# First half of the output product between the halves of the attention-output product, and a new order inside an attention turn

## The chip, the cores and the metric

The kernel runs on one core of one Trainium2 chip, as one program and one launch. The metric is device time in microseconds (us), from runs of the whole kernel. Engines are named as in the profile: PE is TensorE, DVE is VectorE, ACT is ScalarE, POOL is GpSimd, SP issues most transfers.

## The reference, cut to what matters

Two transformer-like layers, one after the other, on a sequence of 1024 tokens by 1024 features, in float32. The change lies in the first:

```python
u = rms_norm(x) @ w_in                   # v, b, c, z, q, k, v_a, z_a, gates
y_a = conv_branch(...) @ w_conv_out      # "co"
o = sliding_window_attention(q, k, v, sinks) * silu(z_a)
y_b = o @ w_attn_out                     # "ao"
merged = sigmoid(g_a) * y_a + sigmoid(g_b) * y_b
x = x + merged @ w_out                   # "wo"
```

The attention has 16 query heads and 4 key/value heads of 64, blocks of 128 queries, each looking at its own block and the one before. The second layer (pooling and gated linear attention, cross attention, a feed-forward part) begins with an RMS norm of x and stays as it is.

## The kernel before, in words

**Numbers.** Each float32 operand of a large product is held as a rounded high part and a low part (the rest); a product is three matmuls (`mm3`, L380): high by high, high by low, low by high. ACT makes high parts, DVE low ones. Activations lie with features on partitions, as 8 tiles of 128 by 512 for each half of the tokens (h = 0, 1). A `dense` (L385) is one weight page of 1024 by 128 times one half: 8 x 3 matmuls into one of three banks `mm`.

**Weights.** `_stream` (L79) lists the weight pages in the order of use, and `Weights` (L229) walks it: SP loads raw pages (`wr`, two buffers, L241), `pf` (L258) has ACT make `wh` (L281, two buffers) and notes the low part, `flush` has DVE make it (`wl`, L345). `get` takes a page and starts the one after.

**Ticks.** All other work lies in Python generators in the list `side`. `tick()` (L178) makes the open low parts of weights and then takes each generator one `yield` further. A `dense` ticks after half of its matmuls, and the loop around it ticks again at its end, so a product is two ticks. This sets the order of instructions on every engine; each engine takes its own in that order and waits where an operand isn't there.

**z and the sums.** After the first norm, `first_two` (L515) multiplies the first two z pages with both halves, then two more z pages follow (L913). Beside that, `sums` (L446) makes the four sums T1 to T4 of the tiles, which the later two-page products of seven block products (`wino`, L398) need; with `fast=True` two of three of its 18 steps end in a yield.

**Attention.** A unit is one pair of key/value heads, one block of queries and two of four query heads of each: 32 units, 16 a half. `attention()` (L1159) gives one turn a tick. In turn i it emits `expo` of unit i-1 (ACT: 4 exponentials, `pr`, L1100), `values` of i-4 (PE into the one bank `o`, L1151; DVE multiplies by the gate, L1155), on odd i `differ` of i-3 (a difference of two value blocks, POOL), `finish` of i-1 (DVE: sum `den` and reciprocal, L1106, L1107; POOL: the division of `pr`, L1108), `turn` of i-2 (PE: 4 transposes, L1128; ACT: `pch`, L1130; DVE: `pcl`, L1131; POOL: masked copies, L1138) and `scores` of i (PE, L1078, into both banks `s`; ACT and DVE copy to `pr`, L1082, L1083; DVE: maximum and scale, L1085 to L1091). Outputs that are complete are split into `oh`, `ol` (L376, L377). Attention starts beside "co" (L1216) and ends beside the first half of "ao".

**ao and wo.** "ao" (L1239) goes over both halves, 8 pages each; behind each product DVE multiplies by the gate (L1250), adds the conv branch (L1251) and ACT and DVE split the merged tile (`mgh`, `mgl`). Gate and conv tiles are loaded one product ahead on SP (`g<-gbd`, `g<-mcd`, L1201). `x` is loaded again on POOL's queue, its first half beside the second half of "ao", its second half behind it. `residual` (L1257) then does "wo": h = 0, 8 products, each added to x (L1267), squared by ACT and summed by POOL (`Norm`, L554), then `norm_thread` (L611) for that half in `side`: beside the second half it makes `xn` (L622), `xnh` and `xnl` a tick; then h = 1.

Of the kernel before, what the change touches and what calls it, by code (L numbers as in the profile page):

```python
# [11 lines left out]
ALU = mybir.AluOpType  # L12
# [6 lines left out]
KT = 8  # L19
# [59 lines left out]
def _stream():  # L79
    st = [("v", 0), ("v", 1)]  # L80
    st += [("z", 0, j) for j in range(4)]
    st += [("pair", ("z", 1, j), ("z", 1, j + 1)) for j in (0, 2)]
    st += [("pair", ("q", p, j), ("q", p, j + 1)) for p in range(2) for j in (0, 2)]
    st += [("pair", ("gb", m), ("gb", m + 1)) for m in range(0, KT, 2)]
    for c in range(KT):
        st += [("pair", ("cc", c), ("cv", c)), ("pair", ("cz", c), ("cb", c))]
    st += [("pair", ("ga", m), ("ga", m + 1)) for m in range(0, KT, 2)]
    st += [("co", m) for m in range(KT)] * 2
    st += [("ao", m) for m in range(KT)] * 2
    st += [("wo", m) for m in range(KT)] * 2  # L90
    st += [("p2", 0)]
    for p in range(2):
        st += [("q2", p), ("k2", p), ("v2", p, 0), ("v2", p, 1)]
    st += [("r2", 0), ("r2", 1), ("p2", 1), ("p2", 2), ("r2", 2), ("p2", 3), ("r2", 3)]
    st += [("wo2", m) for m in range(KT)] * 2
    for m in range(KT):
        st += [("xq", m), ("mk", m), ("mv", m // 4, m % 4)]
    st += [("xq", m) for m in range(KT)]
    st += [("xo", m) for m in range(KT)] * 2
    for f in range(NFF):  # L100
        st += [("fg", f), ("fv", f)] if f < FF_STD else [("pair", ("fg", f), ("fv", f))]
    for g in range(len(FF_GROUPS)):
        st += [("fd", g, m) for m in range(KT)]
    return st
# [12 lines left out]
def _body(es, tc, nc, wp, vec, xT, memT, gk2, pw, cst, out, dbg):  # L117
# [19 lines left out]
    def tp(s, dt=F32, shape=(P, HT)):  # L137
        return tpool.tile(list(shape), dt, name=nm(s), tag="tp")
# [68 lines left out]
    class Page:  # L207
        def __init__(self, his, los):
            self.his, self.los, self.n = his, los, 1024 // len(his)
# [233 lines left out]
        for tag in ("s", "s", "o"):  # L443
            T.matmul(ps(tag), hi[:, :P], hi, start=True, stop=True)

    def sums(t, X, hts, fast=False):  # L446


        at = {"T1": (0, 0), "T2": (4, 1), "T3": (0, 1), "T4": (4, 0)}
        order = ("T1", "T2", "T3", "T4")  # L450
        his, los = {}, {}

        def u(name, k):
            return t[at[name][0] + k, at[name][1]]

        def hi(name, k):
            his[name, k] = hts[name](name, F32R)
            S.copy(his[name, k], u(name, k))

        def lo(name, k):  # L460
            los[name, k] = hts[name](name, F32R)
            V.tensor_tensor(los[name, k], u(name, k), f(his[name, k]), ALU.subtract)
            if k == 3:
                X[name] = [(his[name, i], los[name, i]) for i in range(4)]

        for i in range(18):
            if 2 <= i and i - 2 < 16:
                j = i - 2
                lo(order[j // 4], j % 4)
            if 1 <= i < 17:  # L470
                j = i - 1
                hi(order[j // 4], j % 4)
            k = i % 4
            if i < 4:
                V.tensor_tensor(u("T1", k), u("T3", k), u("T1", k), ALU.subtract)
                V.tensor_tensor(u("T3", k), u("T3", k), u("T2", k), ALU.subtract)
            elif i < 8:
                V.tensor_tensor(u("T2", k), u("T2", k), u("T1", k), ALU.subtract)
            elif i < 12:
                while (4 + k, 0) not in t:  # L480
                    yield
                V.tensor_tensor(u("T4", k), u("T4", k), u("T2", k), ALU.subtract)
            if not fast or i % 3:
                yield

    def reload(items, s, first=4, per=2, lag=3):

# [24 lines left out]
            evac(dense(w, act, h), h)  # L512
            tick()

    def first_two(na, nb, act, ea, eb, spare=False):  # L515

        a = W.get(na)
        ea(dense(a, act, 0), 0)
        tick()
        b = W.get(nb, pf=False)  # L520
        eb(dense(b, act, 0), 0)
        tick()
        while None in [x[1] for x in act]:
            tick()
        if spare:
            W.pf(spare=True)
        o = dense(a, act, 1)
        if not spare:
            W.pf()
        ea(o, 1)  # L530
        tick()
        eb(dense(b, act, 1), 1)
        tick()
# [18 lines left out]


    class Norm:  # L554
        def __init__(self):
            self.acc = None

        def add(self, x, eng=V):
            sq = tp("sq")[:, :x.shape[-1]]
            S.activation(sq, x, AF.Square)  # L560
            if self.acc is None:
                self.acc = sq
            else:
                eng.tensor_tensor(self.acc, self.acc, sq, ALU.add)  # L564
# [70 lines left out]
    def grid(n):  # L635
        return [[None, None] for _ in range(n)]
# [204 lines left out]
    def hT_sums():  # L841
        for k in range(4):
            ht_in(k, hp)
        while None in [x[1] for x in hT]:
            yield
        side.append(ht_rest())
        yield from sums(ht, XB, {"T1": hp, "T2": hp, "T3": hq, "T4": hq}, True)

    def ht_rest():
        while len(kd) < 8 or len(vd) < 4:  # L850
# [58 lines left out]
        wino((na, nb), X, lambda x: evac(0, 0, x), c22, c12, lambda y: evac(1, 0, y))  # L909

    side.append(hT_sums())
    first_two(("z", 0, 0), ("z", 0, 1), hT, *[lambda o, h, j=j: z_out(0, j, h, o) for j in range(2)])
    for j in (2, 3):  # L913
        both(("z", 0, j), hT, lambda o, h: z_out(0, j, h, o))
    while "T1" not in XB:
# [243 lines left out]
    def attention():  # L1159
        units = [Unit(p, h, b, half) for h in range(2) for p in range(2) for b in range(4) for half in range(2)]  # L1160
        n = len(units)
        todo = []
        dv = None
        for _ in range(5):
            yield
        for i in range(n + 4):
            if 0 <= i - 1 < n:
                units[i - 1].expo()
            if 0 <= i - 4 < n:
                units[i - 4].values(dv)  # L1170
                if i % 8 == 3:
                    u = units[i - 4]
                    todo += [(u.p, j, u.h) for j in range(4)]
            if i % 2 and 0 <= i - 3 < n and units[i - 3].n:
                dv = units[i - 3].differ()
            if 0 <= i - 1 < n:
                units[i - 1].finish()
            if 0 <= i - 2 < n:
                units[i - 2].turn()
            if i < n:  # L1180
                units[i].scores()
            if i in (8, 16):
                side.append(att_in(i // 16, 1))
            if todo:
                p, j, h = todo.pop(0)
                osp[4 * p + j][h] = split(oT[p][j][h], "o")
            yield
        while todo:
            p, j, h = todo.pop(0)
            osp[4 * p + j][h] = split(oT[p][j][h], "o")  # L1190
            yield
# [42 lines left out]
        gate_in(gbi, gbd, m, h)  # L1234
        gate_in(cin, mcd, m, h)

    xs = grid(KT)
    ao_in(0, 0)
    for h in range(2):  # L1239
        for m in range(KT):  # L1240
            w = W.get(("ao", m))
            ao_in(m + 1, h)
            if h and m >= 4:
                for i in (0, 1):
                    load_x(0, 2 * (m - 4) + i, nc.gpsimd)
            while None in [osp[c][h] for c in range(KT)]:
                tick()
            o = dense(w, osp, h)
            t = gbi[m, h]
            V.tensor_tensor(t, t, o, ALU.mult)  # L1250
            V.tensor_tensor(t, t, cin[m, h], ALU.add)  # L1251
            mgs[m][h] = split(t, "mg")
            tick()
    for kt in range(KT):
        load_x(1, kt, nc.gpsimd)

    def residual(wname, act, gname, nxt, fast=True, norm=None, between=None, away=None, back=None):  # L1257

        for h in range(2):
            nrm = Norm()  # L1260
            for m in range(KT):
                w = W.get((wname, m))
                if back is not None:
                    for i in range(3) if m == h == 0 else (m + 2,):
                        back(*((h, i) if i < KT else (h + 1, i - KT)))
                o = dense(w, act, h)
                V.tensor_tensor(xs[m][h], xs[m][h], o, ALU.add)  # L1267
                nrm.add(xs[m][h], V if m == KT - 1 else G)
                tick()
            if norm is not None:  # L1270
                side.append(norm([nrm.acc], h))
            else:
                side.append(norm_thread([nrm.acc], xs, gname, h, nxt, fast and h == 1, 1 + (h and not fast),
                                        away))
            if between is not None and h == 0:
                between()

    gr = tp("gr", shape=(P, KT, 16))  # L1280
# [1 line left out]
    gw = tp("gw", F32R, (P, KT, 32))  # L1282
    S.copy(gw[:, :, 0:16], gr)
    V.tensor_tensor(gw[:, :, 16:32], gr, f(gw[:, :, 0:16]), ALU.subtract)
    xn = grid(KT)
    residual("wo", mgs, "norm_mix", xn)


    gl = [None, None]
# [773 lines left out]
```

## Time and profile before

| | us |
|---|---|
| median of 3 runs | 2409.21 |
| lowest, highest run | 2407.96, 2411.95 |
| the profiled execution | 2407.34 |
| its span, first to last instruction | 2405.6 |
| PE busy in the span | 2366.1 |
| DVE, ACT, POOL busy | 1487.5, 1009.5, 577.8 |
| mean granted clock of PE | 0.995 of full |

Busy times overlap, and PE's ends are modelled, so a stretch is judged by the idle time before a matmul and by what ended it. In a row of the timeline the first number is the start from the span's beginning, the second how long it lasted; in brackets stands the engine's idle time before it and what ended that. [...]

### The profile page before, as it was taken

The page shows a single profiled execution, that of the slowest core. Times are in us where ns is not written, and L with a number is a line of the kernel's source. Part 1 is how long each engine was busy: PE and PEld are TensorE (multiplying, and loading weights), DVE is VectorE, ACT ScalarE, POOL GpSimd, SP SyncE. Part 2 cuts the span into 40 slices and gives each one's busy share as a digit, 9 for nine tenths or more (in the row PEclk, how much of TensorE's full clock was granted, in tenths as well). Part 3 has the DMA queues.
Part 4 walks back from the last instruction along what each step waited for, and adds up shares of the span by engine and source line. Part 5 has one row for each costly group of instructions (what it writes and reads, how often), then busy time and mean ns, then how long its engine had stood idle before and what let it go on. Part 6 is the DMA issues. An engine that isn't in the chain of part 4 may idle for free.

```text
span 2405.6 us, 30929 instructions
## 1 busy us (share of the span) xinstructions
PE 2366.1 (98%) x11574; PEld 1952.4 (81%) x11574; DVE 1487.5 (62%) x2317; ACT 1009.5 (42%) x1869; POOL 577.8 (24%) x554
## 2 busy tenths in 40 slices
PE   8999999999999999999999999999999999999998
PEld 8788888888887787887888888888888888888887
DVE  7744346666537997555445556455798888873435
ACT  5444433333346664334322334443555555552112
POOL 3235433333303552121001120001233333310003
PEclk9999999999999999999999999999999999999999
DMA  4533322122247534621100245322422222245222
GB/s 166 181 126 135 124 84 71 62 70 70 84 170 260 184 135 150 210 90 50 39 28 29 88 127 179 97 83 91 160 88 79 79 84 79 93 139 167 84 78 93
DMA packets 107510, 264.97 MB, mean 110 GB/s; under 512 B 12096, under 2 KB 14560, under 8 KB 107360
## 3 DMA queue, kind: packets, MB, share of 16 engines
q1 hardware_dynamic: 104880, 256.70, 31.3%
q0 software_dynamic: 1936, 5.77, 0.7%
q8 instruction: 91, 1.49, 0.2%
q10 hardware_dynamic: 544, 0.52, 0.1%
q14 instruction: 59, 0.48, 0.1%
HBM read 203.18 MB, written 59.77 MB: 109 GB/s over the span
## 4 chain that ended last, share of the span: by engine, by line
PE 88%; DVE 6%; ACT 3%; DMA 1%; issue 1%; POOL 0%; SPq 0%; DVEq 0%; POOLq 0%; ACTq 0%
PE psmm L381 14%; PE psmm L383 13%; PE psmm L382 13%; PE pss L410 6%; PE pss L412 5%; PE pss L411 5%; PE psmm L410 4%; PE psmm L412 4%; PE psmm L411 4%; PE pst L410 2%; PE pst L412 2%; PE pst L411 2%; PE pso L410 2%; PE pso L412 2%; PE pso L411 2%
## 5 line engine op out<-in xcount | busy, mean ns | idle before, releaser
L345 DVE TENSOR_TENSOR wl<-wr,wh 128x1024 fp32r<-128x1024 f32 (+1 forms) x147 | 180.3, 1226 | 97.7 <-ACT wh L281 97.5
L410 PE MATMUL pss<-T,wsh 128*128 128x512 f32 x588 | 232.0, 395 | 0.1
L412 PE MATMUL pss<-T,wsl 128*128 128x512 f32 x588 | 230.1, 391 | 0.0
L411 PE MATMUL pss<-T,wsh 128*128 128x512 f32 x588 | 229.4, 390 | 0.0
L330 DVE TENSOR_TENSOR wsl<-ws,wsh 128x512 fp32r<-128x512 f32 x196 | 208.3, 1103 | 33.4 <-ACT wsh L312 32.4
L564 POOL TENSOR_TENSOR sq<-sq,sq 128x512 f32<-128x512 f32 (+1 forms) x58 | 70.9, 1222 | 608.7 <-ACT sq L560 605.1
L281 ACT CAST wh<-wr 128x1024 fp32r<-128x1024 f32 (+1 forms) x147 | 148.2, 1008 | 149.7 <-PE psmm L382 128.5
L298 POOL TENSOR_TENSOR ws<-wr 128x512 f32<-128x512 f32 x49 | 69.8, 1425 | 567.5 <-DMA wr<-in_wp_dram 459.0
L381 PE MATMUL psmm<-xnh,wh 128*128 128x512 f32 x448 | 179.3, 400 | 5.0 <-ACT wh L281 5.0
L383 PE MATMUL psmm<-xnh,wl 128*128 128x512 f32 x448 | 175.9, 393 | 0.7 <-DVE wl L345 0.7
L382 PE MATMUL psmm<-xnl,wh 128*128 128x512 f32 x448 | 175.5, 392 | 0.0
L410 PE MATMUL psmm<-xnh,wh 128*128 128x512 f32 x392 | 153.9, 393 | 0.0
L412 PE MATMUL psmm<-xnh,wl 128*128 128x512 f32 x392 | 153.2, 391 | 0.0
L411 PE MATMUL psmm<-xnl,wh 128*128 128x512 f32 x392 | 152.6, 389 | 0.0
L410 PEld LDWEIGHTS pss<-T,wsh 128*128 128x128 f32 x588 | 110.4, 188 | 25.6 <-DVE cb L990 2.4
L412 PEld LDWEIGHTS pss<-T,wsl 128*128 128x128 f32 x588 | 110.3, 188 | 25.2
L411 PEld LDWEIGHTS pss<-T,wsh 128*128 128x128 f32 x588 | 110.4, 188 | 23.6
L383 PE MATMUL psmm<-fh,wl 128*128 128x512 f32 (+1 forms) x300 | 116.0, 387 | 1.1 <-DVE wl L345 1.1
L560 ACT ACTIVATE sq<-x 128x512 f32<-128x512 f32 (+1 forms) x80 | 47.1, 588 | 164.7 <-DVE x L1267 110.4
L381 PE MATMUL psmm<-fh,wh 128*128 128x512 f32 (+1 forms) x300 | 115.9, 386 | 0.0
L382 PE MATMUL psmm<-fl,wh 128*128 128x512 f32 (+1 forms) x300 | 115.9, 386 | 0.0
L302 DVE TENSOR_TENSOR wl<-wr,wh 128x1024 fp32r<-128x1024 f32 x49 | 66.0, 1346 | 70.8 <-ACT wh L296 70.8
(453 smaller groups left out, 6231.7 us busy)
## 6 DMA issues: line engine op xcount, KB each, us to landing
wr<-in_wp_dram SPq DMA_DIRECT2D x238, 512.0 KB, 3.7
act<-fa SPq DMA_DIRECT2D x44, 256.0 KB, 2.1
fr<-act SPq DMA_DIRECT2D x44, 256.0 KB, 4.4
wr<-in_wp_dram SPq DMA_DIRECT2D x24, 384.0 KB, 3.1
xd<-x SPq DMA_DIRECT2D x32, 256.0 KB, 4.4
x<-xd SPq DMA_DIRECT2D x32, 256.0 KB, 4.0
x<-in_xT_dram SPq DMA_DIRECT2D x16, 256.0 KB, 5.2
zd<-z SPq DMA_DIRECT2D x16, 256.0 KB, 2.0
```

What stands on the lines that cost most here:

```text
L281: S.copy(hi[:, :n], raw[:, :n])
L298: G.tensor_tensor(sg[0], a21, a22, ALU.add)
L302: V.tensor_tensor(l12, r1, f(h12), ALU.subtract)
L330: V.tensor_tensor(lo, raw, f(hi), ALU.subtract)
L345: V.tensor_tensor(lo, raw, f(hi), ALU.subtract)
L381: T.matmul(out_ap, lh, rh, start=first, stop=False)
L382: T.matmul(out_ap, lh, rl, start=False, stop=False)
L383: T.matmul(out_ap, ll, rh, start=False, stop=last)
L410: T.matmul(o, lh, rh, start=first and kt == 0, stop=False, skip_group_check=True)
L411: T.matmul(o, lh, rl, start=False, stop=False, skip_group_check=True)
L412: T.matmul(o, ll, rh, start=False, stop=kt == 3, skip_group_check=True)
L564: eng.tensor_tensor(self.acc, self.acc, sq, ALU.add)
```

## The change

In the stream of pages the order ao (both halves), wo (both halves) becomes ao, wo, ao, wo, and the loop calls `residual` for one half at a time. The first half of x is loaded on SP beside the first half of ao, and the squares of that half lie in the larger pool. A turn of attention opens with `finish` of unit i-2; `turn` moves to i-3, `differ` to i-4, `values` to i-5; beyond turn 23 every odd turn is followed by a tick without one. `sums` loses its fast form, and the z products fetch the third page one product earlier (`ahead`).

```diff
-    st += [("ao", m) for m in range(KT)] * 2
-    st += [("wo", m) for m in range(KT)] * 2
+    st += ([("ao", m) for m in range(KT)] + [("wo", m) for m in range(KT)]) * 2
...
-    def sums(t, X, hts, fast=False):
+    def sums(t, X, hts):
...
-            if not fast or i % 3:
-                yield
+            yield
...
-    def first_two(na, nb, act, ea, eb, spare=False):
+    def first_two(na, nb, act, ea, eb, spare=False, ahead=False):
...
         b = W.get(nb, pf=False)
+        if ahead:
+            W.pf()
         eb(dense(b, act, 0), 0)
...
         o = dense(a, act, 1)
-        if not spare:
+        if not spare and not ahead:
             W.pf()
...
-            sq = tp("sq")[:, :x.shape[-1]]
+            sq = self.tile("sq")[:, :x.shape[-1]]
...
-        for i in range(n + 4):
+        for i in range(n + 5):
+            if 0 <= i - 2 < n:
+                units[i - 2].finish()
             if 0 <= i - 1 < n:
                 units[i - 1].expo()
-            if 0 <= i - 4 < n:
-                units[i - 4].values(dv)
-                if i % 8 == 3:
-                    u = units[i - 4]
+            if 0 <= i - 5 < n:
+                units[i - 5].values(dv)
+                if i % 8 == 4:
+                    u = units[i - 5]
                     todo += [(u.p, j, u.h) for j in range(4)]
-            if i % 2 and 0 <= i - 3 < n and units[i - 3].n:
-                dv = units[i - 3].differ()
-            if 0 <= i - 1 < n:
-                units[i - 1].finish()
-            if 0 <= i - 2 < n:
-                units[i - 2].turn()
+            if i % 2 == 0 and 0 <= i - 4 < n and units[i - 4].n:
+                dv = units[i - 4].differ()
+            if 0 <= i - 3 < n:
+                units[i - 3].turn()
             if i < n:
                 units[i].scores()
...
             yield
+            if i > 23 and i % 2:
+                yield
...
     for h in range(2):
         for m in range(KT):
             w = W.get(("ao", m))
             ao_in(m + 1, h)
-            if h and m >= 4:
+            if h == 0 and m >= 4:
                 for i in (0, 1):
-                    load_x(0, 2 * (m - 4) + i, nc.gpsimd)
+                    load_x(0, 2 * (m - 4) + i)
...
             mgs[m][h] = split(t, "mg")
             tick()
+        if h == 0:
+            residual("wo", mgs, "norm_mix", xn, halves=(0,), sq=hp)
     for kt in range(KT):
         load_x(1, kt, nc.gpsimd)
...
-    residual("wo", mgs, "norm_mix", xn)
+    residual("wo", mgs, "norm_mix", xn, halves=(1,))
```

## Rows read from the trace of the kernel before

**Rows 1.** The page: busy time, share and instructions of each engine.

```profile
PE 2366.1 (98%) x11574; PEld 1952.4 (81%) x11574; DVE 1487.5 (62%) x2317; ACT 1009.5 (42%) x1869; POOL 577.8 (24%) x554
```

**Rows 2.** Waits of PE over the span: us in total, times, longest.

```profile
PE psmm L381 <- ACT wh L281: 5.0, 1, 5.0
...
PE pst L1128 <- POOL pr L1108: 2.3, 3, 1.2
```

**Rows 3.** By stretch: us, busy PE PEld DVE ACT POOL, clock, DMA share, GB/s.

```profile
77.80:88.80 11.00, 11.00 (x51) 8.92 (x49) 10.76 (x16) 6.58 (x10) 1.75 (x1) 1.00 0.53 207
93.91:99.18 5.27, 5.23 (x12) 3.64 (x13) 1.80 (x2) 3.41 (x6) 0.00 (x0) 0.50 0.71 239
727.85:797.33 69.48, 62.01 (x367) 47.03 (x366) 59.42 (x161) 45.81 (x150) 25.08 (x35) 0.94 0.66 236
797.33:899.56 102.23, 102.23 (x611) 82.03 (x610) 93.90 (x262) 69.73 (x239) 61.11 (x90) 0.99 0.45 155
899.56:928.49 28.93, 24.54 (x110) 18.47 (x109) 22.41 (x57) 15.16 (x45) 12.84 (x19) 0.94 0.22 76
918.38:921.79 3.41, 3.41 (x12) 2.67 (x11) 2.81 (x6) 0.98 (x2) 3.29 (x4) 0.50 0.08 12
960.00:1000.00 40.00, 39.70 (x176) 32.52 (x175) 24.17 (x30) 11.01 (x14) 6.94 (x13) 1.00 0.78 262
```

**Rows 4.** Timelines of SP, ACT and PE around the third z page.

```profile
60.48 0.33 SPq L241 DMA_DIRECT2D wr<-in_wp_dram  x1
...
92.81 1.04 ACT L281 CAST wh<-wr 128x1024 fp32r<-128x1024 f32 x1
...
93.91 0.79 PE L381 MATMUL psmm<-xnh,wh 128*128 128x512 f32 x1 [4.96 <-ACT wh L281]
```

**Rows 5.** Timelines of DVE and ACT, one turn near the start of attention.

```profile
741.52 0.77 DVE L1083 COPY_PREDICATED pr<-iC,pss 128x256 f32<-128x256 uint8 x2
...
745.79 0.16 DVE L1106 TENSOR_TENSOR den<-den,sd 128x4 f32<-128x4 f32 x1 [1.05 <-ACT pr L1100]
...
746.26 0.69 DVE L1131 TENSOR_TENSOR pcl<-pst,pch 128x512 fp32r<-128x512 f32 x1
746.87 0.77 DVE L1083 COPY_PREDICATED pr<-iC,pss 128x256 f32<-128x256 uint8 x2
...
745.66 0.57 ACT L1130 CAST pch<-pst 128x512 fp32r<-128x512 f32 x1
```

**Rows 6.** Waits of DVE in 727.85 to 797.33: us, times, longest.

```profile
DVE den L1106 <- ACT pr L1100: 4.4, 4, 1.6
```

**Rows 7.** Timeline of PE at the seam of the halves of co.

```profile
787.30 0.47 PE L1151 MATMUL pso<-pch,vh 128*128 128x512 f32 x1 [2.54 <-ACT pr L1100]
```

**Rows 8.** One line's instructions, 797.33 to 899.56: count, ns min/median/max, first and last.

```profile
L1078 PE MATMUL pss<-kh,qh x72: 272/328/386, 802.1 to 899.1; 64*128 64x256 f32 x72
```

**Rows 9.** Timeline of DVE beside wo's second half, with the norm.

```profile
1066.22 0.69 DVE L1267 TENSOR_TENSOR x<-x,psmm 128x512 f32<-128x512 f32 x1
1066.83 0.74 DVE L622 SCALAR_TENSOR_TENSOR xn<-x,vt,pst 128x512 f32<-128x512 f32 x1
...
1071.66 0.69 DVE L1267 TENSOR_TENSOR x<-x,psmm 128x512 f32<-128x512 f32 x1
```

**Rows 10.** Timeline of DVE beside ao's first half, behind attention's last turn.

```profile
932.89 0.69 DVE L1250 TENSOR_TENSOR g<-g,psmm 128x512 f32<-128x512 f32 x1 [1.02 <-PE psmm L383]
...
934.99 0.69 DVE L377 TENSOR_TENSOR mgl<-g,mgh 128x512 fp32r<-128x512 f32 x1 [0.69 <-ACT mgh L376]
...
936.46 1.22 DVE L345 TENSOR_TENSOR wl<-wr,wh 128x1024 fp32r<-128x1024 f32 x1 [0.18 <-ACT wh L281]
...
938.33 0.69 DVE L1250 TENSOR_TENSOR g<-g,psmm 128x512 f32<-128x512 f32 x1
```

**Rows 11.** Timeline of DVE at the start of ao's second half.

```profile
961.57 0.69 DVE L1250 TENSOR_TENSOR g<-g,psmm 128x512 f32<-128x512 f32 x1 [2.59 <-DMA g<-gbd]
```

**Rows 12.** The page: issues of one kind, KB each, median us to landing.

```profile
x<-in_xT_dram SPq DMA_DIRECT2D x16, 256.0 KB, 5.2
```

More of the change, by code (lines that the diff above doesn't have):

```diff
@@ L554, in _body, with __init__ @@
     class Norm:
-        def __init__(self):
-            self.acc = None
+        def __init__(self, tile=None):
+            self.acc, self.tile = None, tile or tp
         def add(self, x, eng=V):
-            sq = tp("sq")[:, :x.shape[-1]]
+            sq = self.tile("sq")[:, :x.shape[-1]]
             S.activation(sq, x, AF.Square)
@@ L846, in hT_sums @@
         side.append(ht_rest())
-        yield from sums(ht, XB, {"T1": hp, "T2": hp, "T3": hq, "T4": hq}, True)
+        yield from sums(ht, XB, {"T1": hp, "T2": hp, "T3": hq, "T4": hq})
     def ht_rest():
@@ L911, in _body @@
     side.append(hT_sums())
-    first_two(("z", 0, 0), ("z", 0, 1), hT, *[lambda o, h, j=j: z_out(0, j, h, o) for j in range(2)])
+    first_two(("z", 0, 0), ("z", 0, 1), hT, *[lambda o, h, j=j: z_out(0, j, h, o) for j in range(2)], ahead=True)
     for j in (2, 3):
@@ L1235, in ao_in, with residual @@
         gate_in(cin, mcd, m, h)
[L1237 to L1242, printed above, removed]
-            if h and m >= 4:
-                for i in (0, 1):
-                    load_x(0, 2 * (m - 4) + i, nc.gpsimd)
[L1246 to L1260, printed above, removed]
+    def residual(wname, act, gname, nxt, fast=True, norm=None, between=None, away=None, back=None,
+                 halves=(0, 1), sq=None):
+        for h in halves:
+            nrm = Norm(sq)
             for m in range(KT):
@@ L1276, in residual @@
                 between()
+    xs = grid(KT)
+    xn = grid(KT)
+    ao_in(0, 0)
+    for h in range(2):
+        for m in range(KT):
+            w = W.get(("ao", m))
+            ao_in(m + 1, h)
+            if h == 0 and m >= 4:
+                for i in (0, 1):
+                    load_x(0, 2 * (m - 4) + i)
+            while None in [osp[c][h] for c in range(KT)]:
+                tick()
+            o = dense(w, osp, h)
+            t = gbi[m, h]
+            V.tensor_tensor(t, t, o, ALU.mult)
+            V.tensor_tensor(t, t, cin[m, h], ALU.add)
+            mgs[m][h] = split(t, "mg")
+            tick()
+        if h == 0:
+            residual("wo", mgs, "norm_mix", xn, halves=(0,), sq=hp)
+    for kt in range(KT):
+        load_x(1, kt, nc.gpsimd)
     gr = tp("gr", shape=(P, KT, 16))
@@ L1284, in _body @@
     V.tensor_tensor(gw[:, :, 16:32], gr, f(gw[:, :, 0:16]), ALU.subtract)
-    xn = grid(KT)
-    residual("wo", mgs, "norm_mix", xn)
+    residual("wo", mgs, "norm_mix", xn, halves=(1,))
     gl = [None, None]
```

## The prediction, made before the changed kernel was timed

> **What bounds the kernel now.** I read the page's engine totals first: TensorE is busy 2366.1 of 2405.6 us [rows 1]. The change removes no matmul, so all it can win is idle time and half-clock time of TensorE, and every place where it moves work must be read for what that work makes TensorE wait for. Second, the list of TensorE's waits: of those in the stretches that the change touches I name one of 5.0 us for ACT's rounding of a weight page and three, 2.3 us in all, for POOL's division in attention [rows 2]. Third, busy time by stretch, which shows where these lie and what the other engines did then [rows 3]: the z products (a clock at 0.50 behind the long wait), the first twelve turns of attention (727.85 to 797.33), the steady turns (TensorE never idle), and the attention's end inside the attention-output product ("ao"), 899.56 to 928.49. Last, the order of instructions inside those stretches.
>
> **Part 1, the z products: page fetched ahead, sums one step a tick.** TensorE stops 4.96 us for `wh` of the third z page [rows 4]. Its raw page was asked for at 60.48, so the data isn't late; ACT makes the copy only at 92.81, because its queue holds roundings of the sums' tiles that wait for DVE, and DVE was busy 10.76 of the 11.00 us ahead [rows 3, 4]. The new code asks for that copy one product earlier (near 72) and its low part at the next tick; and the sums take one step a tick, at most two subtractions and a low part, three operations of about 0.65 us where a half product lasts 2.72 (half of the period in part 4). So the wait goes, with the half clock after it: 5.27 us at 0.50 cost 2.6 [rows 3]. Together 4.96 + 2.6 = 7.6. The sums now need 18 ticks instead of 12, and their last sum is used by the seventh product of the first pair, whose tick is about the nineteenth: just in time; I leave 0.1 for it. **Gain 7.5** (bounds 4.5 to 7.8: at the low end ACT still runs one product late).
>
> **Part 2, the order inside a turn.** A turn gives scores of unit i, exponentials of i-1, and so on. In the old order DVE stands 1.05 us at `den` for ACT's exponentials, 4.4 us in four such waits, and TensorE's transposes wait for the division behind it [rows 2, 5, 6]. In the new order the division is of a unit whose exponentials ended a turn ago, so both waits go. But the next copy into `pr` (741.52, then 746.87: 5.35 us a turn) doesn't start behind `den`; it starts behind `pcl`, which needs ACT's `pch`, which stands in ACT's queue behind the same exponentials [rows 5]. That loop (exponentials, `pch`, `pcl`, copy, maximum, exponentials) isn't cut by the change. The first twelve turns go by it, and by turns in which DVE has more than a turn's work: DVE is busy 59.42 of 69.48 us, ACT 45.81, and at the seam of the conv-output product ("co"), where two turns have no product beside them, TensorE waits up to 2.54 us [rows 3, 7]. The wait is late elsewhere: at the output bank instead of at the division. The loop saves one `pch` and `pcl`, about 0.6 (the transposes start a turn later), while one output product and one set of transposes (about 1.2 us) leave this stretch for one that TensorE fills anyway. **Cost 0.6** (bounds: gain 4.4, all of DVE's waits at `den` [rows 6]; cost 2).
>
> [...]
>
> **Part 3, the extra yields, and ao with attention beside it.** In the steady turns TensorE is busy throughout: 102.23 us hold 18 turns (72 of the score matmuls counted, four a turn), 5.68 each, with DVE at 93.90 of 102.23 [rows 3, 8]. In ao DVE gets 1.4 us more per product (an addition and a low part), and TensorE loses 28.93 - 24.54 = 4.39, and 3.41 us at 0.50 another 1.7 [rows 3]. With the new yields two turns of every three ticks are attention's: two full turns of DVE's 4.3 us (5.2, which is 93.90 / 18, less half a weight page and half a gate product), three halves of ao's 3.2, and two splits of 0.65 make 14.7 us where TensorE has 14.0; so DVE falls back by under 2 us, twice, and catches up once the scores are through. I leave 1.7 of the 6.1. **Gain 4.4** (bounds 2 to 6.1).
>
> **Part 4, the order ao, wo, ao, wo** ("wo" is the output product). The norm of the first half used to run beside wo's second half; now it runs beside ao's second half. Beside wo each product costs DVE one addition, and with the norm there its rows are full but even: from one addition at 1066.22 over `xn` to the next at 1071.66 is a product's 5.44 us, 24 matmuls of 0.227 [rows 9]. Beside ao the chain is longer. Without the norm: gate product at 932.89, addition, 0.69 us waiting for ACT's `mgh`, low part at 934.99, one more low part of attention (`ol`), `wl` at 936.46, another `ol`, and the next gate product at 938.33, already 5.44 us after the first [rows 10]. The norm puts two operations of that size, `xn` and `xnl`, where each `ol` stood, and ACT rounds `xnh` before `wh`, so `wl` waits for it. By those rows: gate product 0, addition 0.72, wait and low part to 2.7, `xn` to 3.45, ACT's `xnh` from 3.55, `wh` to 5.1, `wl` to 6.3, `xn` and `xnl` to 7.6. So 7.6 us a product where TensorE has 5.44. The eight steps of the norm touch products 1 to 5; three full periods lose 2.17 each (6.5), the edges 0.4, and the norm's broadcast on TensorE (0.9) covers part: 6.0. TensorE is at `wl` or `wh` then; the clock may fall too, as it did at 918.38 amid such losses [rows 3], but here the clock would eat into waits that are there anyway. **Cost 6.0** (bounds 0.3, if only the edge counts, to 9 with a gate load late once).
>
> **Edits at nothing.** The first half of x is loaded on SP instead of POOL, two tiles behind each of four weight and gate loads; POOL would be busy there with attention. SP's own next load waits for `wl` anyway, and the cover gone would cost a late gate tile, 2.59 us as at 961.57 [rows 11]. The second half of x is asked for where it was, behind ao on POOL, but wo's second half now follows at once: its first tile is wanted a product (5.44) later, and such a load lands in 5.2 [rows 12]; two further banks for products cover a few us more. The residual's squares in another pool: the second half of ao ends with no more live tiles than now (two halves of merged tiles were held, now one and the norm's). At the two seams ao to wo the last merged tile is ready about 2.8 us after its product (gate product to the end of its low part [rows 10]), and wo's first product reads it after 21 matmuls of 0.227 us, 4.8 us.
>
> **Sum.** -7.5 + 0.6 - 4.4 + 6.0 = -5.3. The profiled execution took 2407.34 us (span 2405.63); it becomes 2402.0. The median of the runs shown is 1.87 above it, so 2403.9. A measurement can tell about 0.2% (4.8 us) from no change: faster is under 2404.4, slower over 2414.0. Forecast and boundary nearly meet.
>
> **The rivals.** (a) **DVE's waits were the loop**: taking them shortens the first turns by 4.4 instead of costing 0.6: 2398.9. For it: DVE stands there; against: the copy starts with `pcl`. 0.15. [...] (b) **The norm beside ao is covered**: `wh` gets ahead of `xnh` on ACT, and part 4 costs nothing: 2397.9. For it: beside wo the same steps cost TensorE nothing; against: the 5.44 us already filled beside ao [rows 10]. 0.15. (c) **Late gate tiles in ao's second half**: DVE bounds products 1 to 5, so each late gate load counts in full; at 2.59 [rows 11] five make 13.0: 2416.9, slower. It decides from 2.0 us late on each, (2414.0 - 2403.9) / 5. For it: 262 GB/s and a DMA share of 0.78 in that stage [rows 3]; against: a quarter of x has left it. 0.06. (d) **The early page doesn't come early**, since one of two `wh` buffers is still held by the values' page: part 1 gains nothing, 2411.4. 0.1. The forecast itself: 0.54.
>
> **How the numbers follow.** The forecast alone spreads by about 5 either way (parts 3 and 4), so a bit over half of it, 0.3, lies under 2404.4 and the rest is no change; (a) and (b) are faster in nine cases of ten, 0.27; (d) is mostly no change. Faster 0.57, same 0.35, slower 0.08. The range reaches from under (a) and (b), with part 4 and 3 a little better, to (d): 2395 to 2411; the forecast's own is 2399 to 2409.
>
> **What would show it.** Right: no wait for `wh` near 88 us and clock 1.00 there; no TensorE wait for the division, but still 5.35 us between the copies into `pr`; TensorE's loss in ao's first half under 2.5 us; in ao's second half 7.6 us between gate products three times, and TensorE waiting for `wl`. Wrong: turns shorter than 5.3 us at the start, ao's second half at 5.44 a product, or gate products waiting for DMA.

## The result, and the profile after

The changed kernel takes 2426.27 us (median of 3 runs, 2422.29 to 2427.25), against 2409.21 before: a ratio of 1.0068, interval [1.0054, 1.0082], 17 us slower. The prediction was 2403.9, with a chance of 0.08 on slower; it was wrong by 22 us and in sign. The profiled execution took 2426.27 us with a span of 2424.6, so it is the median itself.

The page and the list of TensorE's waits in the changed kernel, for [rows 1, 2]:

```profile
PE 2377.3 (98%) x11574; PEld 1954.1 (81%) x11574; DVE 1477.4 (61%) x2317; ACT 1010.5 (42%) x1869; POOL 565.5 (23%) x546
```

```profile
PE pso L1151 <- DVE o L1155: 9.0, 9, 2.8
...
PE pso L1151 <- ACT dvh L1120: 6.6, 11, 1.0
PE psmm L382 <- DVE wl L344: 4.5, 7, 1.1
PE psmm L380 <- ACT wh L280: 2.7, 3, 0.9
```

The wait of 5.0 us for `wh` at the third z page is gone, and so are the transposes' waits for POOL's division. Both were forecast. What is new is the second line: the output products wait eleven times for `dvh`, ACT's rounding of the difference between two value blocks. No row of before showed such a wait.

By stretch, with the columns of [rows 3], the last three being the stretches at half clock in attention and at its end (the kernel before has one of 10.24 us in attention too, from 788.67, and the one at 918.38):

```profile
88.80:98.80 10.00, 10.00 (x46) 8.29 (x45) 8.88 (x15) 6.99 (x12) 0.00 (x0) 1.00 0.84 291
727.85:797.33 69.48, 60.12 (x331) 44.92 (x330) 53.31 (x154) 44.46 (x150) 24.23 (x35) 0.93 0.63 215
797.33:899.56 102.23, 99.07 (x559) 75.75 (x558) 78.08 (x233) 62.85 (x212) 47.70 (x74) 1.00 0.42 142
782.97:793.21 10.24, 7.29 (x27) 5.46 (x28) 8.49 (x24) 6.93 (x21) 3.23 (x6) 0.50 0.40 129
919.51:922.92 3.41, 3.41 (x19) 2.61 (x18) 3.27 (x9) 0.56 (x2) 0.83 (x2) 0.50 0.02 6
936.57:943.40 6.83, 6.16 (x16) 4.83 (x17) 4.02 (x9) 2.31 (x4) 4.78 (x9) 0.50 0.29 92
```

The z products now run at full clock without a stop. In attention DVE is *less* busy than before (53.31 of 69.48 us where it had 59.42 [rows 3]) and yet TensorE does fewer matmuls in the same time. The steady turns, in which TensorE had never been idle, now have gaps, and fewer of them fit: 64 of the counted score matmuls where [rows 8] has 72, so 16 turns instead of 18, 6.4 us each instead of 5.68:

```profile
L1078 PE MATMUL pss<-kh,qh x64: 273/330/389, 798.5 to 897.4; 64*128 64x256 f32 x64
```

One such turn shows why. Three fences of the changed kernel's timelines: POOL, ACT and DVE in the same turn.

```profile
843.08 1.04 POOL L1108 TENSOR_TENSOR pr<-pr,den 128x512 f32<-128x512 f32 x1 [2.30 <-DMA ql<-qdl]
844.08 0.46 POOL L1116 TENSOR_TENSOR pwr<-vh,vh 128x128 f32<-128x128 f32 x1
...
845.15 0.46 POOL L1118 TENSOR_TENSOR pwr<-pwr,vl 128x128 f32<-128x128 f32 x1
```

```profile
844.04 0.19 ACT L1100 ACTIVATION_READ_ACCUMULATOR pr<-pr,nmx,rq 128x1 f32 x1
845.64 0.30 ACT L1120 CAST dvh<-pwr 128x128 fp32r<-128x128 f32 x1 [1.41 <-POOL pwr L1118]
845.85 0.58 ACT L1130 CAST pch<-pst 128x512 fp32r<-128x512 f32 x1
```

```profile
834.64 0.77 DVE L1083 COPY_PREDICATED pr<-iC,pss 128x256 f32<-128x256 uint8 x2
...
839.99 0.77 DVE L1083 COPY_PREDICATED pr<-iC,pss 128x256 f32<-128x256 uint8 x2
...
842.63 0.15 DVE L1106 TENSOR_TENSOR den<-den,sd 128x4 f32<-128x4 f32 x1
842.82 0.18 DVE L1107 RECIPROCAL den<-den 128x4 f32<-128x4 f32 x1
...
846.46 0.69 DVE L1131 TENSOR_TENSOR pcl<-pst,pch 128x512 fp32r<-128x512 f32 x1 [2.59 <-ACT pch L1130]
847.07 0.77 DVE L1083 COPY_PREDICATED pr<-iC,pss 128x256 f32<-128x256 uint8 x2
```

Read them in this order. POOL stands 2.30 us idle, then divides as soon as DVE's `den` (842.63) and its reciprocal (842.82 to 843.00) are done, and only then subtracts the value blocks, three operations of 0.46. (The bracket of that division names a load of `ql`, which the division doesn't read; most of the other turns' divisions are put down to `den`.) ACT has finished its exponentials at 844.2 but its next instruction is `dvh`, so it stands until 845.64; `pch` is behind it in ACT's queue, `pcl` waits for `pch` on DVE (2.59 us), and the next copy into `pr` waits behind `pcl`. From copy to copy this turn takes 7.08 us (839.99 to 847.07); the one before it, without a difference, took 5.35. In the kernel before the same three operations stood ahead of the division. POOL did them right after the previous turn's selects (the masked copies), while it would otherwise have idled, and ACT's `dvh` followed the exponentials (at 849.36) with no wait. The timelines before, of POOL and of ACT:

```profile
846.62 0.46 POOL L1116 TENSOR_TENSOR pwr<-vh 128x128 f32<-128x128 f32 x1
...
847.70 0.79 POOL L1118 TENSOR_TENSOR pwr<-pwr,vl 128x128 f32<-128x128 f32 x1
...
850.96 1.04 POOL L1108 TENSOR_TENSOR pr<-pr,den 128x512 f32<-128x512 f32 x1 [0.78 <-DVE den L1107]
```

```profile
849.27 0.19 ACT L1100 ACTIVATION_READ_ACCUMULATOR pr<-pr,nmx,rq 128x1 f32 x1
849.36 0.28 ACT L1120 CAST dvh<-pwr 128x128 fp32r<-128x128 f32 x1
```

The list of waits of all engines in the changed kernel gives the sums; ACT's 13 waits fall in 13 of the 14 turns that have a difference, while `pcl` waits in other turns as well:

```profile
DVE pcl L1131 <- ACT pch L1130: 40.8, 23, 2.6
...
ACT dvh L1120 <- POOL pwr L1118: 24.4, 13, 2.5
```

That became theory A: the place in POOL's queue. Theory B was my part 4, the norm beside ao, at a higher price; theory C was the extra yields.

In the expectations, a stretch's "loss" is worked out from the starts of TensorE's matmuls: the spacing of successive starts beyond the median spacing of their shape, summed over the stretch.

### The profile page after: what moved, and what is told of

It is laid out like the page before. It is cut to its first block, busy times and chain, and to the rows that moved or that the text cites. A ratio compares the mean times of both kernels' runs of the same rounds, so it can differ in the third digit from the quotient of the medians.

```text
span 2424.6 us, 30885 instructions
## 1 busy us (share of the span) xinstructions
PE 2377.3 (98%) x11574; PEld 1954.1 (81%) x11574; DVE 1477.4 (61%) x2317; ACT 1010.5 (42%) x1869; POOL 565.5 (23%) x546
## 4 chain that ended last, share of the span: by engine, by line
PE 85%; DVE 6%; ACT 3%; DMA 2%; issue 2%; POOL 2%; SPq 0%; POOLq 0%; DVEq 0%; ACTq 0%
PE psmm L380 13%; PE psmm L382 13%; PE psmm L381 13%; PE pss L409 6%; PE pss L411 5%; PE pss L410 5%; PE psmm L409 4%; PE psmm L411 4%; PE psmm L410 4%; PE pst L409 2%; PE pst L411 2%; PE pst L410 2%; PE pso L409 2%; PE pso L411 2%; PE pso L410 2%
```

## The experiments

All were timed against the kernel before on the same chip; its median was 2409.1 to 2409.5 in the four sittings.

**One part at a time.** `z_alone` is the kernel before with the z part of the change only.

> The kernel before with part 1 alone (page fetched one product earlier, sums one step a tick). Both theories of the loss leave this part as predicted: 7.8 us less than the kernel before (its stretch from 60 to 120 us lost 7.8 us of TensorE time before the change and 0.0 after it), so about 2401.5. A result within 2 us of the kernel before would say that what is won at the z products is given back later, and that all my sums by stretch are off.

Measured: 2403.02, ratio 0.9970 [0.9958, 0.9981]. Part 1 wins 6.5 us.

`turn_alone` is the kernel before with the new turn, without the yields.

> The kernel before with the new order of the turn alone (division two back, values five back), without the extra yields and with the old order of the output products. Theory A (the division now stands ahead of the three value differences in POOL's queue, so ACT's cast dvh waits for POOL on every second turn, and the turn loop behind it is longer): slower by about 12 us (the loss of the stretch from 720 to 900 us was 8.8 before and 21.2 after), 2421, with ACT waits of 1.4 to 2 us ahead of dvh. Theory B (the loss is in the order ao, wo, ao, wo and its norm; the turn costs what I predicted): slower by 0.6, at most 2, 2410 to 2411. Theory C (the extra yields stretch the attention and are the cause): no more than 2 us slower here either.

Measured: 2427.22, ratio 1.0068 [1.0055, 1.0081], 17.7 us slower, with 22.5 us of ACT waiting for POOL at `dvh`. The turn's order alone makes a loss as large as the whole; B and C fall as explanations of it. It is more than the 12 us that I read off one stretch: from 720 to 900 us the loss is indeed about 12 us above that of the kernel before, and from 900 to 960, where the longer turns run on inside ao, about 7 more. The clock has a small part: attention's half-clock stretch lasts 13.65 us (from 790.43) instead of 10.24.

`after_old_turn` is the changed kernel with the old loop body:

```diff
-        for i in range(n + 5):
-            if 0 <= i - 2 < n:
-                units[i - 2].finish()
...
+        for i in range(n + 4):
+            if 0 <= i - 1 < n:
+                units[i - 1].expo()
...
```

> The changed kernel with the turn's old order put back; the extra yields, the order ao, wo, ao, wo and the z part stay. Theory A: the 12 us of the turn go, and with the shorter turns 4 us of the attention's end inside ao: faster than the changed kernel by 12 to 20 us, about 2410. Theory B: the loss of the output products stays, 2424 to 2426. Theory C (extra yields): stays at 2420 or over.

Measured: 2405.87, ratio 0.9985 [0.9976, 0.9994]; 20.4 us come back.

**Only the place in POOL's queue.** `diff_first` keeps the division two back and the values five back, and issues the difference's three POOL operations ahead of the division (`rounded` is the cast and the low part, cut from `differ`):

```diff
...
         for i in range(n + 5):
+            new = i % 2 == 0 and 0 <= i - 4 < n and units[i - 4].n
+            if new:
+                d = units[i - 4].differ()
             if 0 <= i - 2 < n:
                 units[i - 2].finish()
...
-            if i % 2 == 0 and 0 <= i - 4 < n and units[i - 4].n:
-                dv = units[i - 4].differ()
+            if new:
+                dv = units[i - 4].rounded(d)
```

> The changed kernel with one thing moved: the three POOL operations of the value difference are issued at the start of the turn, ahead of the division, as they stood on POOL's queue in the kernel before; the cast dvh and the low part dvl stay where they are, and division two back, values five back stay. Theory A (POOL's queue order is the cause): ACT's waits ahead of dvh go, and with them 8 to 12 us of the turn and up to 4 us in ao: 2410 to 2418. Rival (the later division and values themselves cost it, by DVE's or ACT's work falling together): within 3 us of the changed kernel, 2423 to 2427, with the waits of TensorE for dvh and for the output bank still there.

Measured: 2404.06, ratio 0.9974 [0.9964, 0.9983]; 22.2 us below the changed kernel, more than A expected. Its timelines of POOL and ACT in such a turn:

```profile
840.64 0.46 POOL L1116 TENSOR_TENSOR pwr<-vh 128x128 f32<-128x128 f32 x1
...
841.72 0.47 POOL L1118 TENSOR_TENSOR pwr<-pwr,vl 128x128 f32<-128x128 f32 x1
843.77 1.04 POOL L1108 TENSOR_TENSOR pr<-pr,den 128x512 f32<-128x512 f32 x1 [1.58 <-DVE den L1107]
```

```profile
844.17 0.18 ACT L1100 ACTIVATION_READ_ACCUMULATOR pr<-pr,nmx,rq 128x1 f32 x1
844.27 0.28 ACT L1123 CAST dvh<-pwr 128x128 fp32r<-128x128 f32 x1
844.46 0.57 ACT L1133 CAST pch<-pst 128x512 fp32r<-128x512 f32 x1
```

The three operations are done 1.58 us before the division starts, and `dvh` follows the exponentials without a gap. In the steady stretch TensorE is never idle, as in the kernel before:

```profile
797.33:899.56 102.23, 102.23 (x605) 82.44 (x604) 86.92 (x244) 68.20 (x227) 50.81 (x80) 1.00 0.45 150
```

**The same mistake in the old kernel.** `swap_before` exchanges two statements of the kernel before:

```diff
-            if i % 2 and 0 <= i - 3 < n and units[i - 3].n:
-                dv = units[i - 3].differ()
             if 0 <= i - 1 < n:
                 units[i - 1].finish()
+            if i % 2 and 0 <= i - 3 < n and units[i - 3].n:
+                dv = units[i - 3].differ()
```

> The kernel before with two statements of the turn swapped and nothing else: the division of the unit one back is issued ahead of the value difference instead of behind it. Theory A (POOL's queue order): the difference's three POOL operations now stand behind a division that waits for ACT's exponentials, so ACT's dvh waits on 14 of the 32 turns for den, division (1.0) and three operations (1.6), some 3 us each, and the loop behind it with it: slower than the kernel before by 20 to 40 us. Rival (the place in POOL's queue is of no weight, the later division and the later values cost the 17 us by what they do on DVE and TensorE): within 3 us of the kernel before.

Measured: 2445.79, ratio 1.0152 [1.0138, 1.0166], 36 us slower. Its waits in 720 to 960 us:

```profile
DVE pcl L1131 <- ACT pch L1130: 46.0, 13, 3.6
ACT dvh L1120 <- POOL pwr L1118: 44.0, 13, 3.6
...
PE pso L1151 <- ACT dvh L1120: 23.3, 13, 2.4
```

Thirteen times up to 3.6 us, as the sum of `den`, division and three operations said. Nothing else was touched, so the place in the queue is shown as a cause by itself, in both kernels.

**Which queue passes it on.** Two runs leave the division ahead of the difference, as the change has it, and move the cast back on ACT's queue: behind `pch` (`dvh_behind`), and behind the scores' copies too (`dvh_last`). The low part moves with it, on POOL's queue behind the masked copies. Both edits in one diff:

```diff
             if 0 <= i - 3 < n:
                 units[i - 3].turn()
+            if new:                           # dvh_behind
+                dv = units[i - 4].rounded(d)
             if i < n:
                 units[i].scores()
+            if new:                           # dvh_last, instead
+                dv = units[i - 4].rounded(d)
```

> The changed kernel with POOL's queue left as it is, the division ahead of the difference, but ACT's cast dvh (and POOL's low part) issued behind the turn's pch and pcl instead of ahead of them. If what costs is that pch stands in ACT's queue behind a dvh that waits for POOL, the loop is freed: 2403 to 2410, as with the difference first. If what costs is POOL's lateness itself (TensorE's output products waiting for the difference), it stays over 2418.

Measured: 2416.36, ratio 1.0029 [1.0017, 1.0040]: between the two answers. The waits in 720 to 960 us say why:

```profile
ACT dvh L1123 <- POOL pwr L1118: 17.3, 13, 1.7
DVE pr L1083 <- ACT pr L1082: 15.6, 12, 1.7
DVE pcl L1134 <- ACT pch L1133: 12.8, 22, 1.8
```

`pch` was freed (DVE's wait at `pcl` fell from 40.8 to 12.8 us; with the difference first it is 13.9), but the copies into `pr` were now behind the waiting cast.

> As the run with dvh behind pch (2416.4), but the cast and its low part issued behind the scores' copies as well, as the last thing of the turn on ACT; POOL's three operations stay behind the division. In that run dvh's wait for POOL stayed (17.3 us) and DVE waited 15.6 us for the copies into pr that now stood behind it. If a waiting dvh costs by whatever stands behind it in ACT's queue, taking it behind both frees the loop: 2402 to 2408. If half of the cost is POOL's lateness itself (the low part dvl late for the output products), it stays at 2414 or over.

Measured: 2409.23, ratio 1.0000 [0.9991, 1.0009], just above the expected band. TensorE's waits that are left in 720 to 960 us:

```profile
PE pso L1154 <- POOL dvl L1125: 4.6, 6, 0.8
PE pso L1154 <- ACT dvh L1123: 4.1, 4, 1.0
```

So of the 22.2 us, taking the cast from ahead of `pch` gives back 9.9 (2426.27 to 2416.36), taking it from ahead of the copies 7.1 (to 2409.23), and 5.2 are left (to 2404.06). What is left shows as output products that wait for `dvh` and `dvl`. How much of that is the late difference itself isn't separated: the cast and the low part came later by the edits too.

**What is left: the norm.** `norm_late` is `diff_first` with the first half's norm started where it ran before, behind ao's second half (its sum of squares is held until then):

```diff
...
+    side.append(norm_thread(kept, xs, "norm_mix", 0, xn, False))
     for kt in range(KT):
         load_x(1, kt, nc.gpsimd)
```

> The kernel with the difference first (2404.1), and the norm of the first half started behind the second half of ao, as it ran in the kernel before, instead of beside it. If the norm beside ao is the loss of 6.0 us that I priced (the stretch from 990 to 1050 us lost 9.3 us there, 0.2 in the kernel before): faster by 6 to 9, 2395 to 2398. If the loss comes from the order ao, wo, ao, wo itself (x tiles late, merged tiles late at the seams): within 2 us of 2404.

Measured: 2394.47, ratio 0.9939 [0.9925, 0.9952], the fastest of all, 9.6 us below `diff_first`. The first fence holds DVE's gate products in ao's second half in the changed kernel, the second in `norm_late`:

```profile
1020.74 0.69 DVE L1275 TENSOR_TENSOR g<-g,psmm 128x512 f32<-128x512 f32 x1 [2.10 <-PE psmm L382]
...
1028.23 0.68 DVE L1275 TENSOR_TENSOR g<-g,psmm 128x512 f32<-128x512 f32 x1
...
1033.36 1.22 DVE L344 TENSOR_TENSOR wl<-wr,wh 128x1024 fp32r<-128x1024 f32 x1 [1.09 <-ACT wh L280]
...
1050.72 0.68 DVE L1275 TENSOR_TENSOR g<-g,psmm 128x512 f32<-128x512 f32 x1
...
1063.03 0.69 DVE L1275 TENSOR_TENSOR g<-g,psmm 128x512 f32<-128x512 f32 x1 [3.60 <-DMA g<-gbd]
```

```profile
998.51 0.69 DVE L1284 TENSOR_TENSOR g<-g,psmm 128x512 f32<-128x512 f32 x1 [1.17 <-PE psmm L382]
1003.95 0.69 DVE L1284 TENSOR_TENSOR g<-g,psmm 128x512 f32<-128x512 f32 x1 [1.17 <-PE psmm L382]
```

With the norm there, four of DVE's periods take 29.98 us (1020.74 to 1050.72), 7.5 each, and `wl` waits for `wh`; without it 5.44, and DVE waits for TensorE. What TensorE loses is read from its own matmuls. In the changed kernel it waits in three of those products, each time once for `wh` and once for `wl`, and then at the seam, in wo's first product, for the last merged tile:

```profile
1033.38 0.50 PE L380 MATMUL psmm<-oh,wh 128*128 128x512 f32 x1 [0.87 <-ACT wh L280]
...
1034.64 0.50 PE L382 MATMUL psmm<-oh,wl 128*128 128x512 f32 x1 [0.53 <-DVE wl L344]
...
1066.32 0.50 PE L380 MATMUL psmm<-mgh,wh 128*128 128x512 f32 x1 [0.98 <-ACT mgh L375]
```

By the spacing of the starts the three products lose 1.95, 1.99 and 1.99 us, one shortly behind them 0.2, and the seam 2.7 (its waits, and the wider spacing behind each). In `norm_late` none of these losses is there.

**The yields and the order.** `no_yields` and `late_no_yields` take the extra yields out of `diff_first` and of `norm_late`:

```diff
             yield
-            if i > 23 and i % 2:
-                yield
```

> The kernel with the difference first (2404.1), without the extra yields. By part 3 as predicted, two turns of attention in three ticks win 4.4 us in ao's first half; by the stretch from 900 to 960 us (7.2 lost before, 3.8 with the difference first) they win 3.4: slower by 3 to 4.5, about 2408. Rival: the gain of that stretch comes from the turn's new order alone, and the yields are worth nothing: 2403 to 2405.

> The kernel with the norm late (2394.5) without the extra yields. By part 3 as predicted the yields win 4.4 in ao's first half: 2398 to 2399. By the run without them (2405.35 against 2404.06, intervals overlapping, 3.5 lost from 900 to 960 us with and without): 2394 to 2396, no difference that can be told.

Measured: 2405.35, ratio 0.9982 [0.9973, 0.9991], against 2404.06; and 2395.85, ratio 0.9944 [0.9932, 0.9957], against 2394.47. Twice some 1.3 us in the expected sense and the intervals overlap: the yields' worth can't be told from nothing, and it isn't 4.4.

`order_back` is `diff_first` with ao, ao, wo, wo and the old residual; `old_turn_late` has the new order with the norm late, and the old turn.

> The kernel with the difference first and the extra yields, but with the old order ao, ao, wo, wo (so its norm of the first half runs beside wo again, as in the run with the norm started late, 2394.5). If the order ao, wo, ao, wo is worth something by itself apart from its norm (part 3: attention's end has ao alone beside it, 7.2 us lost there in the kernel before, 3.6 with the norm late): slower than 2394.5 by 3 to 4.5, 2398 to 2399. Rival: the order is worth nothing, and what it did was only to move the norm: 2393 to 2396.

> The z part, the order ao, wo, ao, wo with the norm late, and the extra yields, with the turn's old order (the run with the old turn gave 2405.9 with the norm beside ao; the norm late won 9.6 us beside the new turn). It closes a table of four: old turn and old order 2403.0 (the z part alone), mended turn and old order 2395.8, mended turn and new order 2394.5. If the new order wins by itself what part 3 said (4.4), and the mended turn wins the same stall in another way: 2395 to 2399. If only the mended turn wins it: 2402 to 2404.

Measured: 2395.76, ratio 0.9944 [0.9931, 0.9956], in the band of the rival, by which the order is worth nothing beside the mended turn; and 2396.91, ratio 0.9949 [0.9936, 0.9963], in the band of a new order that wins by itself. The table of four, all with the z part (the first without the yields):

| | old turn | new turn, difference first |
|---|---|---|
| order ao, ao, wo, wo (norm beside wo) | 2403.0 | 2395.8 |
| order ao, wo, ao, wo, norm late | 2396.9 | 2394.5 |

Either one wins 6 to 7 us; the second then adds 1.3 to 2.4, with intervals that overlap, so it can't be told from nothing. The gains don't add, as if both remove largely the same stall. In the profiles part of it is clock: attention's half-clock stretch near 780 us lasts 10.24 us in `z_alone` and 3.41 in `order_back`. How the rest divides wasn't settled.

## Why the prediction was wrong, step by step

**Part 1** (gain 7.5) was right: 6.5 measured alone, and `wh` is copied at 82.40 instead of 92.81. It came later than the "near 72" that I wrote, but early enough. Rival (d) is out.

**Part 2** (cost 0.6, bounds a gain of 4.4 and a cost of 2) is the step that failed: 17.7. Its first half held: no transposes wait for the division, and copies into `pr` in the steady turns without a difference still start 5.35 to 5.63 us apart, so nothing has shortened the loop that I named. The sentence that failed is "That loop (exponentials, `pch`, `pcl`, copy, maximum, exponentials) isn't cut by the change". It wasn't cut, but it was lengthened. I followed the moved division on DVE's queue and to its users, and did not ask what it is put ahead of on POOL's own queue. Three operations of 0.46 were there, whose result ACT needs in the middle of that very loop. The bound of 2 us left them out: counted on 14 turns, a division and three operations (some 2.6 us) behind `den` were up to 36 us to set against whatever slack ACT has there; the waits came to 24.4. That work waits behind what stands ahead of it the runs show on two queues: on ACT's `pch` stood behind a `dvh` that waited 1.41 us; on POOL's the three operations won 22.2 us when they went ahead of the division (`diff_first`) and cost 36 when they went behind it (`swap_before`). I had followed this on DVE's queue and not on POOL's.

Rival (a) was closer than I allowed, once the difference is first: 7.2 us were won beside the old order (with the yields), not 0.6 lost. Its mechanism is not shown by that: in that run (`order_back`) the copies of turns without a difference are still 5.35 us apart or more.

**Part 3** (gain 4.4, bounds 2 to 6.1) had about the right size for the wrong cause. The new order and the yields won 6.1 beside the old turn (2403.0 to 2396.9), but the yields alone, to which I put the gain down, gave nothing that can be told beside the mended turn (beside the old one they weren't tried alone). In the changed kernel the gain was lost again: the longer turns ran on inside ao (attention's last output products start at 959 us, at 929 in the kernel before), where the clock fell to 0.50 at 919.51, as it had at 918.38 before [rows 3], and once more at 936.57.

**Part 4** (cost 6.0, bounds 0.3 to 9) had the mechanism right and the period to a tenth, 7.5 us a product against 7.6, and TensorE waited for `wh` and `wl` as said; it was too small: 9.0 to 9.6 (2405.9 to 2396.9, 2404.1 to 2394.5). The three products lost 5.9 where I had 6.5, and the edge 0.2 where I had 0.4. (DVE has a fourth long period, but the first of the four, from 1020.74, costs TensorE nothing: DVE was ahead there, 2.10 us idle for TensorE.) Two terms were mis-sized. The seam to wo, costed at nothing, lost 2.7 in the changed kernel. And the norm's broadcast on TensorE, which I let cover 0.9, covered nothing, since it comes ahead of the first wait (in the changed kernel its 8 matmuls start at 1020.54 and last 1.05, and the first wait ends at 1033.38). Rival (b) is out. Rival (c) came true for one tile, and not for one of its five products: the load for ao's last gate product landed 7.3 us after its issue, where the median of these loads is 4.0. It was 3.60 us late, and its merged tile held up wo's first product; a gate load late once was the upper end of my bounds. POOL asked for the second half of x from 1045.2 to 1057.2, around that load's issue at 1055.65; in `norm_late` it did so from 986.3 to 994.8, and no gate product waits for a load there. That the loads of x made the gate tile late is likely by these times; no run moved them alone.

**The sum.** The terms measured alone, -6.5 + 17.7 - 6.1 + 9.0 = 14.1, come near the 17.1 that the change cost, but aren't independent. That `diff_first` took 2404.06, my 2403.9, is no merit of the sum: parts 2 and 3 share a gain there, and part 4 takes more than I gave it.

## What to carry to other kernels

When a step is moved, list for every engine it uses what its instructions now stand ahead of, and who waits for those. Here a division that started late was moved ahead of three independent operations of 0.46 us on POOL's queue. That took them out of idle time, and ACT, which needs their result, passed the delay to what stood behind it there: in the changed kernel 24.4 us of waits at `dvh` and 40.8 at `pcl`, and with the turn alone a kernel 17.7 us slower. Before adding two gains, ask whether they remove the same stall.

## What the runs showed of the hardware

In `swap_before` TensorE's clock fell in stretches that had kept it: the steady turns, at a mean of 0.99 before [rows 3], have stretches at 0.50, beside waits for `dvh` (13 from 720 to 960 us, the longest 2.4). In one of them, which begins just behind a wait of 1.96 us for `dvh`, TensorE is not idle at all (busy 3.41 of 3.41 us), so the price there doesn't lie in idle time. What a matmul took at such a clock the z products of the kernel before show: those of 128x512 start 0.43 us apart at 0.50 (97.04 to 97.47) and 0.23 us at 1.00 (87.88 to 88.11). The first line is that stretch; below it stands the whole of 720 to 960 us, in `swap_before` and then in the kernel before:

```profile
860.50:863.91 3.41, 3.41 (x19) 2.54 (x19) 3.27 (x9) 1.72 (x7) 1.01 (x2) 0.50 0.00 1
```

```profile
720.00:960.00 240.00, 208.01 (x1097) 156.01 (x1096) 165.44 (x469) 130.66 (x428) 90.50 (x139) 0.94 0.44 153
```

```profile
720.00:960.00 240.00, 228.14 (x1256) 179.83 (x1256) 198.64 (x506) 141.47 (x446) 101.30 (x148) 0.97 0.52 182
```

So the waits cost more here than their length: the 13 waits of TensorE for `dvh` there sum to 23.3 us, the kernel lost 36, and the half-clock time in this stretch rose from 13.65 to 30.7 us. By an estimate, the 17 us more at half speed are worth some 8.5.

The other fact is on POOL. Its subtraction of 128x128 (L1118) took 0.99 us on average from 735 to 900 us in the kernel before and 0.47 with the difference first, with the same shapes and the same place ahead of the division. The timelines show what differs: in the kernel before 12 of the 14 took 0.79 to 1.33 us, each while DVE ran a subtraction of 128x512 or 128x1024 that makes `ol`, `ycl` or `wl`, with neither operand in the kernel's PSUM pool. In 13 of the 14 with the difference first no such operation ran beside it for more than its last 0.06 us, and they took 0.46 to 0.47; the one that took 0.79 had DVE's `mgl` beside it. The DVE operation was longer there too: the `ol` at 847.22, beside the 0.79 at 847.70 shown above, took 0.95 us where the ones at 841.64 and 853.53 took 0.69. The POOL operation that had started ahead of that `ol` kept its time (L1117 at 847.16, 0.46), and in `dvh_behind` POOL kept 0.46 beside DVE's `pcl`, one operand of which (`pst`) lies in that pool. This is what coincides in the traces; no run moved it alone, and why the operations take longer was not shown. It changed no time that I could see: at 850.96 the division behind that subtraction still waited 0.78 us for `den`.
